# Fewer, larger units of half-array products in a mixer layer, and selector products filled from 36 to 128 rows

## The chip, the core and the metric

The kernel runs on one core of one Trainium2 chip. Its engines work side by side, each through its own list of instructions in order: TensorE (PE in the profile; its weight loads are PEld), VectorE (DVE), ScalarE (ACT), GpSimd (POOL), and SyncE (SP), which issues most DMAs. The metric is the device time of one execution in microseconds (us). Three runs of the kernel before took 302.65, 302.69 and 302.83 us.

## The reference

One decoder layer on a sequence of 512 tokens of width 1024, all float32:

- RMS norm of x, then one projection `h @ w_in` to 4616 columns, and at the end one projection `y @ w_out` back to 1024, added to x.
- A matrix-memory group (mLSTM) of 4 heads of width 128: causal convolution and SiLU on q and k, input and forget gates, a stabilised recurrence over time, a norm per head, a SiLU gate.
- An attention group of 8 heads of width 64: norm of q and k, a linear penalty on distance, softmax over all earlier keys, a SiLU gate. With 512 tokens and blocks of 256, the "top 3 blocks" are all the past there is, so this is plain causal attention.

```
s = q . k * scale - slope * distance      (masked to the past)
p = softmax(s);   o = p @ v
y = concat(h_mlstm * silu(z_ml), o * silu(z_at)) @ w_out;   return x + y
```

## The kernel before

**Products in parts.** A float32 operand of the large products is split into a high part (`whi`, `xh`) and a remainder (`wlo`, `xl`), and a product becomes three fast ones, high x high, high x low and low x high. ACT makes the high part of a weight tile, DVE the remainder; PE then streams 512 columns per product through the full array of 128 rows x 128 columns. "Wide product" below means one of these.

**Attention.** `g_attn` works on a pair of heads, 2p and 2p+1, that lie in rows 0 to 63 and 64 to 127 of the same tiles (four tiles named `br`: high and low parts of q and k). A *query tile* is 128 query rows; there are four. For tile i, `g_tile` (L861) takes two PSUM banks, one for each head, and issues six score products, three for each head in turn: rows 0 to 63 of the array for the one, rows 64 to 127 for the other, so that the two run at the same time. Width is 256, 256, 384 and 512 columns for tiles 0 to 3. In `g_soft` DVE adds the penalty and takes the row's extreme (a custom instruction, named CUSTOM_DVE_ANT_0), ACT exponentiates, DVE inverts the sum, POOL scales. PE turns the probabilities over (128x128 products with the identity, `ident`), and four steps of probabilities times values (L923) follow: 64 columns of the array for each head, two heads at a time. These are plain float32 products, and each has two records in the trace.

**Matrix memory.** `g_mlstm` (L982) needs for each head a row of running maxima copied to all 128 partitions. It does this as a product of `sel` (a matrix of zeros and ones) with `mrow2` (L989): both have 36 rows, of which rows 0 to 3 and 32 to 35 matter. There are four such selector products.

**What sets the order.** At the start the program writes constants by hand: POOL makes `ident`, `dist`, clears `mrow2` and the edge of `xp`; DVE clears a tile for ten warm-up products of zeros on PE and adds up `sel` from pieces of `ident`. These are issued in the order of the code. From `nc.on = True` (L647) on, instructions are only recorded. `Schedule` then gives each a cost and a list of what it must follow (tiles read and written; a PSUM bank counts as a whole), places them engine by engine, backwards and forwards twelve times (`place`, L308), and issues them in the order of the best placing. What is recorded between `nc.bundle = []` and `nc.bundle = None` is one unit (L262): it is placed as one and nothing of PE's comes in between. All instructions of the recorded part carry the line of their issue, L258, so they are told apart by tile names. `tables` (L292) keeps ACT's Exp, SiLU and Sigmoid work in the order of the recording and puts a table load between.

**Banks.** `banks` has eight PSUM banks; `KEEP = 3` is what a recorded program leaves free for the main stream of wide products.

Of the kernel before, what the change touches and what calls it, by code (L numbers as in the profile page):

```python
# [11 lines left out]
F32 = mybir.dt.float32  # L12
# [5 lines left out]
P = 128  # L18
# [171 lines left out]
class Schedule:  # L190
# [61 lines left out]
    def add(self, eng, name, fn, args, kw):  # L252
        aps = [a for a in (*args, *kw.values()) if isinstance(a, bass.AP)]
        out = kw.get("out", args[0] if args else None)
        outs = [r for r in (self.region(a) for a in (out, kw.get("accum_out")) if a is not None) if r]
        ins = [r for r in (self.region(a) for a in aps if a is not out and a is not kw.get("accum_out")) if r]
        dma = name.startswith("dma")
        call = lambda: fn(*args, **kw)  # L258
        op = {"eng": eng, "fn": [call], "cost": self.cost(eng, name, out, ins, args, kw), "n": len(self.ops),
              "table": next((self.TABLES[a] for a in args if isinstance(a, AF) and a in self.TABLES), 0) if name == "activation" else 0,  # L260
              "pre": {}}
        if self.bundle is not None:  # L262

            if not self.bundle:
                self.bundle.append(op)
            elif op is not self.bundle[0]:
                self.bundle[0]["cost"] += op["cost"]
                self.bundle[0]["fn"].append(call)
            op = self.bundle[0]
        if op["n"] == len(self.ops):  # L270
            self.ops.append(op)
        done = op
        if dma:
            size = 4.0
            for d in out.shape:
                size *= d
            done = {"eng": "dma", "fn": None, "cost": size / 524288.0 * (2900.0 if kw.get("accum_op") else 1480.0), "n": len(self.ops),
                    "table": 0, "pre": {op["n"]: 0.0}}
            self.ops.append(done)
        for reg, write in [(r, False) for r in ins] + [(r, True) for r in outs]:  # L280
            log = self.log.setdefault(reg[0], [])
            for r, w, o in log:
                if (w or write) and r[1] < reg[2] and reg[1] < r[2] and r[3] < reg[4] and reg[3] < r[4]:
                    if o["n"] in (op["n"], done["n"]):
                        continue
                    lat = self.LAT[o["eng"]] if o["eng"] != eng else 0.0 if eng == "tensor" else self.OWN if w else 0.0
                    op["pre"][o["n"]] = max(op["pre"].get(o["n"], 0.0), lat)
            if write:
                log[:] = [e for e in log if e[2] in (op, done) or not (reg[1] <= e[0][1] and e[0][2] <= reg[2] and reg[3] <= e[0][3] and e[0][4] <= reg[4])]
            log.append((reg, write, done))  # L290
# [97 lines left out]
def hybrid_layer(ctx: ExitStack, tc: tile.TileContext, xT, x, w_in, w_out, smalls, out):  # L388
# [11 lines left out]
    def sb(name, shape, dtype=F32):  # L400
        return const.tile(shape, dtype, name=name)
# [10 lines left out]
    def pe(t=0.0, cond=None):  # L412
        return (t, cond, True)
# [8 lines left out]
    def mm(out_, lhsT, rhs, start=True, stop=True):  # L422
        n = 1
        for d in rhs.shape[1:]:
            n *= d
        plan.now += n / 2.4 if rhs.dtype == F32R else 4 * max(n, 128) / 2.4
        nc.tensor.matmul(out_, lhsT=lhsT, rhs=rhs, start=start, stop=stop, skip_group_check=True)
# [192 lines left out]
    rstd = sb("rstd", [P, NT])  # L620
    acol = sb("acol", [P, NT, 4])
    emcol = sb("emcol", [P, NT, 4])
    mrow2 = sb("mrow2", [36, S], F32R)
    nc.gpsimd.memset(mrow2.bitcast(F32), 0.0)
    sel = sb("sel", [36, MLH, P], F32R)
    for h in range(MLH):
        nc.vector.tensor_tensor(sel[:, h], ident[0:36, h:h + 1].to_broadcast([36, P]),
                                ident[0:36, 32 + h:33 + h].to_broadcast([36, P]), op=ALU.add)
    xpt = sb("xp", [P, 2, S + 4])
    nc.gpsimd.memset(xpt[:, :, 0:3], 0.0)  # L630
# [216 lines left out]
    def g_attn(p, qh, ql, kh, kl, t0):  # L847
        rank = 5 + p / 100
        yield when(lambda: b2.ok() and b5.ok(2) and (p < 2 or 2 * p - 3 in pts))
        eh, prs = b2.get(), [b5.get() for _ in range(2)]  # L850

        te = pool.tensor_scalar(eh, dist, 2.0 ** -(2 * p + 1), 0.0, op0=ALU.mult, op1=ALU.add)
        mn, sums, rec = ([tiny(NT) for _ in range(2)] for _ in range(3))
        done = {"p": [0, 0], "t": [0, 0]}
        at = [t0, t0]

        def finish(key, u, t):
            at[u] = max(at[u], t)
            done[key][u] += 1

        def g_tile(i):  # L861
            n = P * (i + 1)
            nn = max(n, 256)
            yield (max(*at, te), lambda: banks.ok(KEEP + 1), True)
            ps = [banks.get() for _ in range(2)]
            ts = slice(i * P, (i + 1) * P)
            now = plan.now
            nc.bundle = []
            for a, b in ((qh, kh), (qh, kl), (ql, kh)):
                for u in range(2):  # L870
                    r = slice(64 * u, 64 * u + 64)
                    mm(ps[u][:, :nn], a[r, ts], b[r, :nn], a is qh and b is kh, a is ql)
            nc.bundle = None
            plan.now = (now + plan.now) / 2
            for u in range(2):
                plan.add(g_soft(u, i, n, ps[u]), rank, plan.now + SLACK)

        def g_soft(u, i, n, ps):
            p_ = prs[u][:, offs[i]:offs[i] + n]
            t_ = dve.tensor_tensor_reduce(p_, ps[:, :n], eh[:, S - n:], scale=-0.5 if u else -1.0, scalar=BIG,  # L880
                                          op0=ALU.add, op1=ALU.min, accum_out=mn[u][:, i:i + 1])
            banks.put(t_, ps)
            yield t_
            yield act.activation(p_, p_, AF.Exp, scale=-1.0, bias=mn[u][:, i:i + 1], accum_out=sums[u][:, i:i + 1])
            have["exp"] += 1
            dve.reciprocal(rec[u][:, i:i + 1], sums[u][:, i:i + 1])
            yield dve.clock + SLACK
            finish("p", u, pool.tensor_scalar(p_, p_, rec[u][:, i:i + 1], 1.0, op0=ALU.mult, op1=ALU.mult))

        def g_pt(u, a, blocks, pt):  # L890
            yield pe_bank(at[u])
            ps = banks.get()
            n = P * len(blocks)
            for b, (i, j) in enumerate(blocks):
                transpose(ps[:, b * P:(b + 1) * P], prs[u][:, offs[i] + j * P:offs[i] + (j + 1) * P], ident)
            yield plan.now + SLACK
            t_ = (act.copy, dve.tensor_copy, act.copy)[a](pt[:, 512 * a:512 * a + n], ps[:, :n])
            banks.put(t_, ps)
            finish("t", u, t_)

        def g_turn(u):
            yield when(lambda: done["p"][u] == NT and b5.ok())
            pt = b5.get()
            for a, blocks in enumerate(([(0, 0), (1, 0), (2, 0), (3, 0)],
                                        [(1, 1), (2, 1), (3, 1), (3, 3)],
                                        [(2, 2), (3, 2)])):
                plan.add(g_pt(u, a, blocks, pt), rank)
            yield when(lambda: done["t"][u] == 3)
            b5.put(plan.now, prs[u])
            pts[2 * p + u] = (pt, [pt[:, 0:512], pt[:, 512:896], pt[:, 1024:1280], pt[:, 896:1024]], at[u])  # L910

        for i in range(NT):
            plan.add(g_tile(i), rank)
        for u in range(2):
            plan.add(g_turn(u), rank + u / 200)
        yield when(lambda: sum(done["p"]) == 2 * NT)
        b2.put(plan.now, eh)
        br.put(plan.now, qh, ql, kh, kl)
        h = 2 * p + 1
        yield when(lambda: h in pts and h - 1 in pts and have["v"] == NT)  # L920
        yield pe_bank(max(pts[h][2], pts[h - 1][2]))
        acc = banks.get()
        for j in range(NT):  # L923
            nc.bundle = []
            for g in (h - 1, h):
                r0 = 64 * (g % 2)
                mm(acc[r0:r0 + 64, j * P:], tv[:, j, g * 64:g * 64 + 64], pts[g][1][j], j == 0, j == NT - 1)
            nc.bundle = None
            plan.now -= 4 * (S - j * P) / 2.4
            if j < NT - 1:  # L930
                yield pe()
        b5.put(plan.now, pts[h - 1][0], pts[h][0])
        yield plan.now + SLACK
        banks.put(dve.tensor_copy(ot[:, h // 2], acc), acc)
        have["at"] += 1
# [694 lines left out]
```

## Time and profile before

| | us |
|---|---|
| median of three runs | 302.69 |
| the profiled execution, its own time | 302.68 |
| its span, first to last instruction | 301.0 |
| PE busy | 296.0 (98%) |
| DVE busy | 214.9 (71%) |
| ACT busy | 169.6 (56%) |
| POOL busy | 67.1 (22%) |

Between span and own time lie 1.7 us. A product's end is modelled and products overlap in the array, so PE counts as busy whenever its products follow each other, whether at full pace or not. Its pace is read from the starts: from one start to the next. The attention of all heads lies between 96.6 and 178.8 us of the span, the selector products between 170.7 and 173.1.

### The profile page before, as it was taken

Reading aid. Unit: us, or ns where it says so; the run is one execution under the profiler, and the core shown is the slowest. Engines: PE = TensorE matmul, PEld = TensorE weight load, DVE = VectorE, ACT = ScalarE, POOL = GpSimd, SP = SyncE. Lnnn points to the kernel's source line nnn. Section 1 sums busy time; section 2 is a strip of 40 time slices with the busy share of each in tenths; the row PEclk is TensorE's granted clock in tenths of the full one; section 3 lists DMA queues with packets and bytes.
Section 4 is the critical chain, followed back from the end, with each engine's and each line's share of the span. In section 5 each row is a group of like instructions: output and inputs, shape, how many; then the busy total and the mean of one; then the engine's idle time right before and its main releaser. Section 6 shows DMA issues by size and latency. Waiting matters only on the chain.

```text
span 301.0 us, 4348 instructions
## 1 busy us (share of the span) xinstructions
PE 296.0 (98%) x1566; PEld 234.9 (78%) x1566; DVE 214.9 (71%) x457; ACT 169.6 (56%) x309; POOL 67.1 (22%) x90
## 2 busy tenths in 40 slices
PE   8999999999999999999999999999999999999995
PEld 3999888888887667767776668888889988888884
DVE  4886996789697675986686784372046767899992
ACT  3685749875537854364554599377032525779500
POOL 4000202149900344002561031000101037121200
PEclk9999999999999999999999999999999999999998
DMA  7994785643134200240001601465518399964434
GB/s 203 396 415 186 191 237 148 121 138 114 58 111 140 71 2 0 70 142 1 1 3 70 209 2 70 70 207 154 131 42 212 102 286 255 247 112 74 71 127 153
DMA packets 13381, 40.19 MB, mean 134 GB/s; under 512 B 1584, under 2 KB 1840, under 8 KB 13360
## 3 DMA queue, kind: packets, MB, share of 16 engines
q1 hardware_dynamic: 10640, 32.05, 30.6%
q0 software_dynamic: 2720, 7.87, 15.3%
q8 instruction: 12, 0.20, 0.3%
q14 instruction: 9, 0.07, 0.1%
HBM read 37.81 MB, written 2.10 MB: 133 GB/s over the span
## 4 chain that ended last, share of the span: by engine, by line
PE 97%; DMA 1%; DVE 0%; SPq 0%; issue 0%
PE bank L258 97%; DMA b<-in_w_in_dram 1%; DVE whi L258 0%; DVE b L258 0%; SPq L258 0%; SPq L381 0%
## 5 line engine op out<-in xcount | busy, mean ns | idle before, releaser
L258 PE MATMUL bank<-wlo,xh 128*128 128x512 f32 (+2 forms) x220 | 71.3, 358 | 0.0
L258 PE MATMUL bank<-whi,xl 128*128 128x512 f32 (+2 forms) x220 | 71.1, 359 | 0.0
L258 PE MATMUL bank<-whi,xh 128*128 128x512 f32 (+2 forms) x220 | 70.9, 362 | 0.1
L258 DVE TENSOR_TENSOR wlo<-raw,whi 128x1024 fp32r<-128x1024 f32 x35 | 42.5, 1218 | 22.3 <-ACT whi L258 22.2
L258 PEld LDWEIGHTS bank<-whi,xh 128*128 128x128 f32 x220 | 38.1, 188 | 8.1 <-ACT xh L258 1.0
L258 PEld LDWEIGHTS bank<-wlo,xh 128*128 128x128 f32 x220 | 38.3, 188 | 6.6 <-issue 0.2
L258 PEld LDWEIGHTS bank<-whi,xl 128*128 128x128 f32 x220 | 38.3, 188 | 6.4
L258 ACT CAST whi<-raw 128x1024 fp32r<-128x1024 f32 x35 | 36.5, 1049 | 11.6 <-PE bank L258 11.5
L258 PE MATMUL bank<-xh,whi 128*128 128x512 f32 x96 | 40.8, 425 | 0.0
L258 PE MATMUL bank<-xl,whi 128*128 128x512 f32 x96 | 39.4, 410 | 0.0
L258 PE MATMUL bank<-xh,wlo 128*128 128x512 f32 x96 | 38.7, 403 | 0.0
L258 PE MATMUL bank<-whi,br 128*128 128x512 f32 x112 | 35.9, 397 | 0.0
L258 POOL TENSOR_SCALAR b<-b,tinies 128x128 f32<-128x128 f32 (+3 forms) x32 | 20.0, 632 | 35.1 <-DVE tinies L258 32.5
L258 PEld LDWEIGHTS bank<-whi,br 128*128 128x128 f32 x112 | 21.0, 188 | 5.0
L258 ACT ACTIVATE b<-b,tinies 128x128 f32<-128x128 f32 (+3 forms) x32 | 17.8, 556 | 11.3 <-DVE tinies L258 11.0
L258 DVE CUSTOM_DVE_ANT_0 b<-bank,b 128x128 f32<-128x128 f32 (+3 forms) x32 | 14.8, 483 | 10.7 <-PE bank L258 10.7
L258 PEld LDWEIGHTS bank<-xh,whi 128*128 128x128 f32 x96 | 18.1, 188 | 5.5 <-issue 1.4
L258 PE MATMUL bank<-wlo,br 128*128 128x512 f32 x56 | 22.2, 400 | 0.0
L258 PEld LDWEIGHTS bank<-xh,wlo 128*128 128x128 f32 x96 | 18.1, 188 | 3.8 <-issue 0.2
L258 PEld LDWEIGHTS bank<-xl,whi 128*128 128x128 f32 x96 | 18.1, 189 | 3.6 <-issue 0.7
L258 POOL TENSOR_TENSOR tinies<-tinies,mhalf 128x8 f32<-128x8 f32 (+1 forms) x12 | 18.9, 1589 | 6.3 <-DVE tinies L258 6.2
L258 PE MATMUL bank<-ident,b 128*128 128x128 f32 (+1 forms) x104 | 19.0, 267 | 0.0
(170 smaller groups left out, 457.2 us busy)
## 6 DMA issues: line engine op xcount, KB each, us to landing
raw<-in_w_in_dram SPq DMA_DIRECT2D x28, 512.0 KB, 3.4
raw<-in_w_out_dram SPq DMA_DIRECT2D x5, 512.0 KB, 4.4
vbuf<-in_x_dram SPq DMA_DIRECT2D x4, 512.0 KB, 7.8
out_dram<-b SPq DMA_DIRECT2D x7, 256.0 KB, 2.1
b<-in_w_in_dram SPq DMA_DIRECT2D x3, 520.0 KB, 7.1
raw<-in_w_out_dram POOLq DMA_DIRECT2D x3, 512.0 KB, 6.3
b<-in_x_dram POOLq DMA_DIRECT2D x6, 256.0 KB, 4.4
tq<-in_xT_dram SPq DMA_DIRECT2D x4, 256.0 KB, 4.9
```

The lines of the kernel that those rows point to most:

```text
L258: call = lambda: fn(*args, **kw)
```

## The change

Three edits. `g_tiles` puts the scores of two query tiles into one unit, (0, 1) and (2, 3); tiles 0 and 1 share one bank for each head (columns 0 to 255 and 256 to 511), tiles 2 and 3 take two banks for each head at once. A shared bank is given back after both reductions have read it. The four steps of probabilities times values become one unit. `sel` and `mrow2` get 128 rows; the new rows are zero, so `sel` is cleared on POOL before DVE adds into its first 36 rows. Besides, the planner charges each unit 190 ns more.

```diff
@@ Schedule.add
             if not self.bundle:
                 self.bundle.append(op)
+                op["cost"] += 190.0
@@ hybrid_layer
-    mrow2 = sb("mrow2", [36, S], F32R)
+    mrow2 = sb("mrow2", [P, S], F32R)
     nc.gpsimd.memset(mrow2.bitcast(F32), 0.0)
-    sel = sb("sel", [36, MLH, P], F32R)
+    sel = sb("sel", [P, MLH, P], F32R)
+    nc.gpsimd.memset(sel.bitcast(F32), 0.0)
     for h in range(MLH):
-        nc.vector.tensor_tensor(sel[:, h], ident[0:36, h:h + 1].to_broadcast([36, P]),
+        nc.vector.tensor_tensor(sel[0:36, h], ident[0:36, h:h + 1].to_broadcast([36, P]),
                                 ident[0:36, 32 + h:33 + h].to_broadcast([36, P]), op=ALU.add)
@@ g_attn
-        def g_tile(i):
-            n = P * (i + 1)
-            nn = max(n, 256)
-            yield (max(*at, te), lambda: banks.ok(KEEP + 1), True)
-            ps = [banks.get() for _ in range(2)]
-            ts = slice(i * P, (i + 1) * P)
+        def g_tiles(tiles):
+            n_banks = 1 if tiles[0] == 0 else 2
+            yield (max(*at, te), lambda: banks.ok(KEEP + 2 * n_banks - 1), True)
             now = plan.now
-            nc.bundle = []
-            for a, b in ((qh, kh), (qh, kl), (ql, kh)):
-                for u in range(2):
-                    r = slice(64 * u, 64 * u + 64)
-                    mm(ps[u][:, :nn], a[r, ts], b[r, :nn], a is qh and b is kh, a is ql)
+            nc.bundle, got = [], []
+            for j, i in enumerate(tiles):
+                n = P * (i + 1)
+                nn = max(n, 256)
+                if j < n_banks:
+                    ps = [banks.get() for _ in range(2)]
+                c0 = 0 if j < n_banks else 256
+                ts = slice(i * P, (i + 1) * P)
+                for a, b in ((qh, kh), (qh, kl), (ql, kh)):
+                    for u in range(2):
+                        r = slice(64 * u, 64 * u + 64)
+                        mm(ps[u][:, c0:c0 + nn], a[r, ts], b[r, :nn], a is qh and b is kh and not c0, a is ql)
+                got.append((i, n, ps, c0))
             nc.bundle = None
...
-            banks.put(t_, ps)
+            left[id(ps)] -= 1
+            if not left[id(ps)]:
+                banks.put(t_, ps)
...
-        for i in range(NT):
-            plan.add(g_tile(i), rank)
+        for tiles in ((0, 1), (2, 3)):
+            plan.add(g_tiles(tiles), rank)
...
         acc = banks.get()
+        nc.bundle = []
         for j in range(NT):
-            nc.bundle = []
             for g in (h - 1, h):
                 r0 = 64 * (g % 2)
                 mm(acc[r0:r0 + 64, j * P:], tv[:, j, g * 64:g * 64 + 64], pts[g][1][j], j == 0, j == NT - 1)
-            nc.bundle = None
             plan.now -= 4 * (S - j * P) / 2.4
-            if j < NT - 1:
-                yield pe()
+        nc.bundle = None
```

The diff leaves the order to the planner, so three places are shown as the built programs have them.

PE, the first scores of heads 0 and 1, before: `br` tiles are q and k, each `bank` a PSUM bank; `xh`, `xl`, `whi0`, `wlo0` belong to a wide product.

```order
L258 MATMUL bank2_82<-xl_107,whi0_108 128x512
L258 MATMUL bank0_80<-br_2_74,br_0_72 128x256
L258 MATMUL bank3_83<-br_2_74,br_0_72 128x256
L258 MATMUL bank0_80<-br_3_75,br_0_72 128x256
L258 MATMUL bank3_83<-br_3_75,br_0_72 128x256
L258 MATMUL bank0_80<-br_2_74,br_1_73 128x256
L258 MATMUL bank3_83<-br_2_74,br_1_73 128x256
L258 MATMUL bank2_82<-xh_106,wlo0_109 128x512
L258 MATMUL bank7_87<-br_2_74,br_0_72 128x384
L258 MATMUL bank5_85<-br_2_74,br_0_72 128x384
L258 MATMUL bank7_87<-br_3_75,br_0_72 128x384
L258 MATMUL bank5_85<-br_3_75,br_0_72 128x384
```

The same place of the change, from the last products of tile 1 over tile 2 into tile 3:

```order
L258 MATMUL bank6_86<-br_3_75,br_0_72 128x256
L258 MATMUL bank4_84<-br_2_74,br_1_73 128x256
L258 MATMUL bank6_86<-br_2_74,br_1_73 128x256
L258 MATMUL bank0_80<-br_2_74,br_0_72 128x384
L258 MATMUL bank3_83<-br_2_74,br_0_72 128x384
L258 MATMUL bank0_80<-br_3_75,br_0_72 128x384
L258 MATMUL bank3_83<-br_3_75,br_0_72 128x384
L258 MATMUL bank0_80<-br_2_74,br_1_73 128x384
L258 MATMUL bank3_83<-br_2_74,br_1_73 128x384
L258 MATMUL bank7_87<-br_2_74,br_0_72 128x512
L258 MATMUL bank5_85<-br_2_74,br_0_72 128x512
L258 MATMUL bank7_87<-br_3_75,br_0_72 128x512
```

Before, a wide product stands between tile 0, tile 1 and tile 2; now all 24 score products of this pair of heads stand in one piece.

PE, the selector products (`mrow2` and `sel`), before:

```order
L258 MATMUL bank1_81<-mrow2_149,sel_151 128x512
L258 MATMUL bank0_80<-ident_124,b5_4_67 128x128 x2
L258 MATMUL bank5_85<-ident_124,b5_4_67 128x128
L258 MATMUL bank3_83<-mrow2_149,sel_151 128x512
L258 MATMUL bank7_87<-mrow2_149,sel_151 128x512
L258 MATMUL bank6_86<-whi0_108,xh_106 128x512
L258 MATMUL bank2_82<-mrow2_149,sel_151 128x512
```

They stand in three pieces, and of the change in two:

```order
L258 MATMUL bank6_86<-whi3_114,xl_107 128x512
L258 MATMUL bank0_80<-mrow2_149,sel_151 128x512
L258 MATMUL bank1_81<-mrow2_149,sel_151 128x512
L258 MATMUL bank7_87<-whi0_108,xh_106 128x512
L258 MATMUL bank7_87<-wlo0_109,xh_106 128x512
L258 MATMUL bank7_87<-whi0_108,xl_107 128x512
L258 MATMUL bank5_85<-mrow2_149,sel_151 128x512
L258 MATMUL bank4_84<-mrow2_149,sel_151 128x512
```

The piece matters less here than the rows: the products now fill the array's 128 rows, as their neighbours do.

POOL, the constants at the start, of the change (before has the same rows without the fill of `sel`, and 36 rows in that of `mrow`):

```order
masks.py:199 AFFINE_SELECT ident<-ident 128x128
L382 MEMSET mhalf 128x8
L382 IOTA dist 128x512
L382 AFFINE_SELECT dist<-dist 128x512
L382 MEMSET one_col 128x1
L382 MEMSET mrow_149 128x512
L382 MEMSET sel 128x512
L382 MEMSET xp 128x2x3
```

DVE at the start, of the change (before has the same rows): the four additions into `sel`, and behind them the first high part of weights.

```order
L382 MEMSET rstdb 128x256
L382 MEMSET warm 128x1
L382 TENSOR_TENSOR sel<-ident 36x128 x4
L258 CAST whi_108<-b_0_63 128x520
L258 SCALAR_TENSOR_TENSOR xl<-tq,sm,xh 128x512
```

The additions read only `ident` before; now they also follow POOL's fill of `sel`, which stands five rows behind `ident` there.

## Rows read from the trace of the kernel before

**Rows 1.** Stretch and its us; busy PE, PEld, DVE, ACT, POOL; clock, DMA share, GB/s.

```profile
96.60:178.80 82.20, 82.20 (x467) 56.67 (x466) 59.53 (x166) 46.98 (x122) 23.16 (x38) 1.00 0.16 52
```

**Rows 2.** Everything that PE waited for: engine, line, releaser, us, times, longest.

```profile
PE bank L381 <- DVE warm L381: 1.2, 1, 1.2
```

**Rows 3.** Chain that ended last, its longest piece: start, us, what.

```profile
5.83 291.52 PE bank L258 x1556
```

**Rows 4.** Timeline of PE, tiles 2 and 3 of heads 2, 3: start, us, what.

```profile
106.10 0.40 PE L258 MATMUL bank<-xh,wlo 128*128 128x512 f32 x1
106.43 0.79 PE L258 MATMUL bank<-br,br 64*128 64x384 f32 x6
107.15 0.50 PE L258 MATMUL bank<-xh,whi 128*128 128x512 f32 x1
107.48 0.39 PE L258 MATMUL bank<-xl,whi 128*128 128x512 f32 x1
...
107.94 0.40 PE L258 MATMUL bank<-xh,whi 128*128 128x512 f32 x1
108.27 0.96 PE L258 MATMUL bank<-br,br 64*128 64x512 f32 x6
109.16 0.50 PE L258 MATMUL bank<-xl,whi 128*128 128x512 f32 x1
109.50 0.39 PE L258 MATMUL bank<-xh,wlo 128*128 128x512 f32 x1
```

**Rows 5.** Timeline of PE, tiles 2 and 3 of heads 6, 7, which adjoin.

```profile
150.77 0.40 PE L258 MATMUL bank<-xh,wlo 128*128 128x512 f32 x1
151.10 1.49 PE L258 MATMUL bank<-br,br 64*128 64x384 f32 x12
152.52 0.50 PE L258 MATMUL bank<-xh,whi 128*128 128x512 f32 x1
152.85 0.39 PE L258 MATMUL bank<-xl,whi 128*128 128x512 f32 x1
```

**Rows 6.** Timeline of PE, the last selector product.

```profile
172.25 0.49 PE L258 MATMUL bank<-whi,xh 128*128 128x512 f32 x1
172.67 0.50 PE L258 MATMUL bank<-mrow,sel 36*128 36x512 f32 x1
173.10 0.50 PE L258 MATMUL bank<-wlo,xh 128*128 128x512 f32 x1
173.44 0.39 PE L258 MATMUL bank<-whi,xl 128*128 128x512 f32 x1
```

**Rows 7.** Timeline of PE, wide products between steps of probabilities times values.

```profile
176.80 0.50 PE L258 MATMUL bank<-whi,xh 128*128 128x512 f32 x1
177.13 0.39 PE L258 MATMUL bank<-wlo,xh 128*128 128x512 f32 x1
```

**Rows 8.** Timeline of POOL at the start.

```profile
3.20 0.29 POOL masks.py:199 TENSOR_SCALAR_AFFINE_SELECT ident<-ident 128x128 f32<-128x128 f32 x1
...
4.88 0.51 POOL L381 MEMSET mrow<- 36x512 f32 x1
5.34 0.38 POOL L381 MEMSET xp<- 128x6 f32 x1
```

**Rows 9.** Timeline of DVE at the start.

```profile
3.52 0.89 DVE L381 TENSOR_TENSOR sel<-ident 36x128 fp32r<-36x128 f32 x4 [2.33 <-POOL ident masks.py:199]
5.16 0.53 DVE L258 CAST whi<-b 128x520 fp32r<-128x520 f32 x1 [0.74 <-DMA b<-in_w_in_dram]
```

**Rows 10.** Timeline of PE, the warm-up products.

```profile
1.24 4.45 PE L381 MATMUL bank<-rstdb 128*128 128x512 bf16 x10 [1.24 <-DVE warm L381]
```

**Rows 11.** Groups by form (count | busy, mean ns | idle before): score reductions, table loads.

```profile
L258 DVE CUSTOM_DVE_ANT_0 b<-bank,b 128x256 f32<-128x256 f32 x8 | 3.2, 422 | 4.2 <-PE bank L258 4.2
L258 DVE CUSTOM_DVE_ANT_0 b<-bank,b 128x128 f32<-128x128 f32 x8 | 2.0, 282 | 1.8 <-PE bank L258 1.8
...
L258 ACT ACT_TABLE_LOAD x4 | 5.1, 1283 | 0.1
```

More of the change, by code (lines that the diff above doesn't have):

```diff
@@ L873, in g_tile @@
             nc.bundle = None
             plan.now = (now + plan.now) / 2
-            for u in range(2):
-                plan.add(g_soft(u, i, n, ps[u]), rank, plan.now + SLACK)
-        def g_soft(u, i, n, ps):
+            left = {}
+            for _, _, ps, _ in got:
+                for u in range(2):
+                    left[id(ps[u])] = left.get(id(ps[u]), 0) + 1
+            for i, n, ps, c0 in got:
+                for u in range(2):
+                    plan.add(g_soft(u, i, n, ps[u], c0, left), rank, plan.now + SLACK)
@@ L879, in g_soft @@
+        def g_soft(u, i, n, ps, c0, left):
             p_ = prs[u][:, offs[i]:offs[i] + n]
-            t_ = dve.tensor_tensor_reduce(p_, ps[:, :n], eh[:, S - n:], scale=-0.5 if u else -1.0, scalar=BIG,
+            t_ = dve.tensor_tensor_reduce(p_, ps[:, c0:c0 + n], eh[:, S - n:], scale=-0.5 if u else -1.0, scalar=BIG,
                                           op0=ALU.add, op1=ALU.min, accum_out=mn[u][:, i:i + 1])
-            banks.put(t_, ps)
+            left[id(ps)] -= 1
+            if not left[id(ps)]:
+                banks.put(t_, ps)
```

## The prediction

> **What bounds the kernel now.** I read the busy times by stretch first, then what PE waited for, then the chain that ended last, and only then the timeline. In the attention's stretch PE has a product in it for 82.20 of 82.20 us while DVE, ACT and POOL have gaps [rows 1]. Over the whole execution PE waited for another engine once, for DVE at the very start [rows 2], and the chain that ended last is one unbroken piece of 1556 products on PE from 5.83 us on [rows 3]. So the time is the sum of PE's steps from one start to the next, plus the moment of its first real product. Everything else can only matter by making PE late.
>
> The steps are not all alike. Wide products next to each other start 0.23 us apart; around scores, which use half of the array's rows each, the steps are longer. Tile 2 and tile 3 of heads 2 and 3 stand alone: wide to score takes 0.33 us (106.10 to 106.43, and 107.94 to 108.27), and the step after the first wide product behind scores 0.33 and 0.34 [rows 4]. The six scores of tile 2 hold PE for 0.72 us and those of tile 3 for 0.89, together 1.61. The same two tiles of heads 6 and 7 happen to stand together and take 1.42 (151.10 to 152.52) [rows 5]. So the trace already holds the change in small: two pieces cost 4 edges and one piece 2.
>
> **The price of one piece.** From the wide product at 106.10 to the one at 107.48 are 1.38 us, less two wide steps of 0.23 leaves 0.92 for tile 2; from 107.94 to 109.50 are 1.56, less the same leaves 1.10 for tile 3: 2.02 [rows 4]. From 150.77 to 152.85 are 2.08, less 0.46 leaves 1.62 for both in one piece [rows 5]. One piece less is worth 0.40 us. It is made of some 0.10 each for the first score, the last score, the step into the piece and the step behind it.
>
> **What the change removes.** Counted over PE's whole order, pieces of scores fall from 15 to 7. The four pairs of heads had 16 units, two of which adjoin; now there are 8 units, two of which adjoin (heads 0 and 1). 8 x 0.40 = 3.2 us.
>
> The selector products stood in three pieces. From the wide product at 172.25 to that at 173.44 are 1.19 us for two wide products and one selector product: three plain steps are 0.69, and 0.50 is left, 0.10 of which is the step behind the piece before it. So a piece of these costs 0.40 too [rows 6]. With 128 rows the products use the array as the wide ones do, and no edge should remain: 3 x 0.40 = 1.2 us.
>
> Of probabilities times values two of the four pairs of heads had their steps in two pieces, now none: 6 pieces become 4. Behind such a piece the first wide step is 0.33 us again [rows 7]; the other edges I price as those of scores, with 0.10 as the lower and 0.40 as the upper end for a piece. I take 0.40, since the one edge seen equals that of scores: 0.8 us (0.2 to 0.8).
>
> The sum of gains is 5.2 us. The number of products is the same, 1474 in both orders, and so are their widths.
>
> **What it adds at the start.** This is where the change costs. Before, DVE's four additions into `sel` began at 3.52 us, 0.03 behind the end of POOL's `ident` (3.20 + 0.29), and were done at 4.41. DVE's next instruction, the high part of the first weights, began at 5.16, when its DMA had landed; it had 0.74 us to spare [rows 8, 9]. Now the additions write into a tile that POOL has to clear first. In POOL's list that fill stands behind the fill of `mrow`, which took from 4.88 to 5.34, where the next one began [rows 8]. So the new fill begins at 5.34 at best. It has as many columns as that of `mrow`, whose 0.51 us I take for it; the trace has no fill of 128 rows and this width, and `xp`'s six columns took 0.38, so it lies between 0.38 and, if time went by rows, four times 0.51, which is 2.0. It ends at 5.85, the additions run from 5.88 to 6.77, and the high part starts at 6.77 in place of 5.16: 1.6 us later (1.5 to 3.1). DVE works in order, so nothing behind can pass. PE's first real product needs that high part, and the 1556 products behind it never wait again, so the whole delay comes through to the end. Queued behind the additions on DVE are, besides that high part, the low parts of x and of the weights, all of which PE takes as they come. On POOL the fill of `xp` and one small instruction come half a microsecond later; nobody waits for them then.
>
> **What is hidden.** A reduction of tile 0 now waits for tile 1 as well, and a shared bank comes free after two reductions of each head instead of one: 2 x (0.28 + 0.42) = 1.4 us of DVE work [rows 11]. In the new order 13 wide products follow the first 24 scores before the next pair of heads takes these banks, 13 x 0.23 = 3.0 us. DVE is idle for 22.7 of the 82.2 us there [rows 1]. I take nothing for it; uncovered it would cost up to 1.4 us at each of four places. ACT's list gets one more table load, 1.28 us [rows 11], since SiLU now stands between the exponentials of two matrix-memory heads and those of the other two. ACT has 35 us free in this stretch [rows 1], and the first turned product of the matrix memory stands 45 wide products (10 us) behind the last selector product; nothing, with 1.3 as the upper end. The last 160 rows of PE's list are the same, so the end should follow PE as before.
>
> **Sum.** 302.68 (the profiled execution, against a median of 302.69) - 3.2 - 1.2 - 0.8 + 1.6 = 299.1 us.
>
> **The rivals.**
>
> *The fill costs nothing* (the additions are early enough all the same, or DVE's first high part is not held): then 302.68 - 5.2 = 297.5. For it speaks only that DVE had 0.74 us to spare; against it that the fill begins 0.18 us after the moment at which that instruction began.
>
> *The clock comes back late.* The ten warm-up products took 4.45 us, 0.43 for 512 columns [rows 10], twice the 0.23 of the wide products later [rows 4]: by their pace they ran at the lower of PE's two levels, 1.2 GHz, and the first real products followed 0.14 us behind them, after which the trace shows the higher pace. Now PE would stand still from 5.69 to about 7.4 us. If a stretch as long as the warm-up then ran at the lower level again, it would lose half of 4.45, 2.2 us: 301.3. For it: the whole warm-up ran at the lower level. Against it: the warm-up itself is unchanged, and the pause is little more than a third of it. The Trainium skill (TensorE: Matmul & The Clock Gate, What's actually happening) says that the throttled state is the default and that activity releases it, which makes idling at this place the dangerous kind. The trace agrees in so far as the ten products did run at half pace.
>
> *Only part of the price goes away*, because a piece with 128 rows of zeros or two tiles in one bank pays its edges all the same: half of the gain, 302.68 - 2.6 + 1.6 = 301.7. Against it are the two adjoining tiles [rows 5].
>
> *Slower: PE waits for the banks.* With four banks for each unit of tiles 2 and 3, and shared ones for 0 and 1, PE could stand at the start of each pair's units until DVE has reduced the tiles before. If PE waits out all the reductions of two shared banks, 1.4 us, twice at each of four pairs of heads, it loses 11.2 us: 310.3. It decides from 3.6 us on, which is 0.9 for each pair. For it: banks are held longer, and DVE is at 72% there. Against it: before, PE never waited for DVE [rows 2], and the planner knows the banks.
>
> **How the numbers follow.** The likeliest case, 299.1 and within 298.4 to 300.1, has 0.63; the fill for nothing 0.09; the late clock, anywhere between 299.7 and 301.3 since the rise may come halfway, 0.16; half of the price 0.05; waits for banks 0.07, of which 0.04 end above the time before. A measurement of this kernel tells about 0.2% (0.6 us) from no change. Faster by more than that needs a time under 302.1: all cases but the waits and a piece of the longest fill, 0.90; within 0.2%: 0.05; slower: 0.05. The range goes from 298.0, which leaves out the fill for nothing, to 301.3, which takes in the late clock and leaves out half of the price and the waits: 0.2 outside.
>
> **What would show it.** In the profile after: PE's first real product at about 7.4 us, with DVE's `sel` additions from 5.9 and the fill of `sel` on POOL just before them; 24, 12, 12, ... score products in seven pieces, and the step into a piece 0.33 as before; a selector product 0.23 us behind its neighbour; all 16 records of a pair's probabilities times values in one piece; PE without a wait between its first product and its last; and a span shorter by 3.5. It would be wrong if the first product still came at 5.8, if products at about 7.4 to 12 us ran at half pace, or if PE waited for DVE between 100 and 110 us.

## The result, and the profile after

Four runs took 298.98, 300.04, 300.50 and 300.50 us, median 300.27, against 302.67 for the kernel before in the same runs: ratio 0.991 (95% interval 0.989 to 0.993). The profiled execution is the one of 298.98, against 302.68 for the profiled one before: 3.7 us less. The other three are 1.1 to 1.5 us longer, and no run of the kernel before is spread like that (302.20 to 302.83). Their mean granted clock is 0.994 in both runs of 300.50 and 0.998 in that of 300.04, against 0.999 in the profiled one; none of the three has a profile.

The chain that ended last, after (start, us, what):

```profile
0.79 1.84 DMA sm<-in_smalls_dram
...
4.83 0.46 POOL mrow L382
5.29 0.46 POOL sel L382
5.75 0.05 POOL xp L382
5.80 0.06 DVE sel L382
...
6.01 0.68 DVE sel L382 x3
6.69 0.35 DVE whi L258
...
7.18 286.48 PE bank L258 x1556
```

Two numbers carry the result. PE's piece is 286.48 us in place of 291.52 [rows 3], 5.04 less for the same 1556 products. And it starts at 7.18 in place of 5.83, 1.35 later, because the chain now runs through POOL's fills and DVE's additions to the first high part of weights; before, that part waited for its DMA [rows 8, 9]. 5.04 - 1.35 is the 3.7. DVE's own timeline shows the additions behind the fills (`xp` is the POOL instruction that follows the fill of `sel`) and the high part right behind them:

```profile
5.78 0.91 DVE L382 TENSOR_TENSOR sel<-ident 36x128 fp32r<-36x128 f32 x4 [4.59 <-POOL xp L382]
6.62 0.41 DVE L258 CAST whi<-b 128x520 fp32r<-128x520 f32 x1
```

PE stood still for 1.5 us in this execution too, and yet it went on at the higher pace: the first eight products took 1.18 us (7.18 to 8.36), as long as before, and the granted clock behind them is 1.00 (below, a stretch with its busy times, clock, DMA share and GB/s).

```profile
7.18 1.19 PE L258 MATMUL bank<-whi,xh 128*128 128x264 f32 x8 [1.50 <-DVE whi L258]
9.00:10.00 1.00, 1.00 (x10) 1.00 (x10) 1.00 (x3) 0.00 (x0) 0.00 (x0) 1.00 1.02 395
```

Timeline of PE after, the first scores (the piece of 24 is both units of heads 0 and 1; that of 12 is tiles 0 and 1 of heads 2 and 3), and below the selector products and the last probabilities times values:

```profile
98.09 0.39 PE L258 MATMUL bank<-xl,whi 128*128 128x512 f32 x1
98.41 2.20 PE L258 MATMUL bank<-br,br 64*128 64x256 f32 x24
100.54 0.50 PE L258 MATMUL bank<-xh,wlo 128*128 128x512 f32 x1
100.87 0.39 PE L258 MATMUL bank<-xh,whi 128*128 128x512 f32 x1
...
103.76 0.98 PE L258 MATMUL bank<-br,br 64*128 64x256 f32 x12
104.67 0.50 PE L258 MATMUL bank<-xh,whi 128*128 128x512 f32 x1
...
174.29 0.62 PE L258 MATMUL bank<-mrow,sel 128*128 128x512 f32 x2
174.75 0.40 PE L258 MATMUL bank<-whi,xh 128*128 128x512 f32 x1
174.98 0.39 PE L258 MATMUL bank<-wlo,xh 128*128 128x512 f32 x1
...
176.70 2.37 PE L258 MATMUL bank<-b,vbuf 128*64 128x512 f32 x16
179.00 0.50 PE L258 MATMUL bank<-whi,xh 128*128 128x512 f32 x1
```

The edges are as dear as before: 98.09 to 98.41 is 0.32, 100.54 to 100.87 is 0.33, as in [rows 4]. There are fewer of them. The first two selector products take 0.46 from 174.29 to 174.75, two plain wide steps, where one took 0.43 and left its neighbours longer [rows 6].

What PE waited for, after (engine, line, releaser: us, times, longest):

```profile
PE bank L258 <- DVE whi L258: 1.5, 1, 1.5
PE bank L382 <- DVE warm L382: 1.2, 1, 1.2
```

The new row against [rows 2] is the start; no wait for a bank or a softmax appears. The attention's stretch again holds a product on PE for its whole length, with DVE 6.6 us busier in the same window than in [rows 1]:

```profile
96.60:178.80 82.20, 82.20 (x489) 61.56 (x488) 66.11 (x174) 48.29 (x119) 28.00 (x36) 1.00 0.20 66
```

### The profile page after: what moved, and what is told of

Read it like the earlier page. It is cut to its first block, busy times and chain, and to the rows that moved or that the text cites. A ratio compares the mean times of both kernels' runs of the same rounds, so it can differ in the third digit from the quotient of the medians.

```text
span 297.3 us, 4346 instructions
## 1 busy us (share of the span) xinstructions
PE 290.9 (98%) x1566; PEld 235.7 (79%) x1566; DVE 215.0 (72%) x457; ACT 170.0 (57%) x310; POOL 74.8 (25%) x91
## 4 chain that ended last, share of the span: by engine, by line
PE 96%; POOL 1%; DMA 1%; DVE 1%; issue 0%; POOLq 0%
PE bank L258 96%; DMA sm<-in_smalls_dram 1%; POOL dist L382 0%; DVE sel L382 0%; POOL mrow L382 0%; POOL sel L382 0%; DVE b L258 0%; DVE whi L258 0%; POOL ident masks.py:199 0%; POOL ident masks.py:197 0%; POOL sm L382 0%; POOL mhalf L382 0%; POOL xp L382 0%; POOL one_col L382 0%; POOLq L382 0%
## 5 line engine op out<-in xcount | busy, mean ns | idle before, releaser
L258 PE MATMUL bank<-xh,whi 128*128 128x512 f32 x96 | 40.2, 419 | 0.0
L258 PE MATMUL bank<-xl,whi 128*128 128x512 f32 x96 | 38.5, 401 | 0.0
L258 POOL TENSOR_SCALAR b<-b,tinies 128x128 f32<-128x128 f32 (+3 forms) x32 | 24.5, 776 | 38.3 <-DVE tinies L258 38.2
L258 POOL TENSOR_TENSOR tinies<-tinies,mhalf 128x8 f32<-128x8 f32 (+1 forms) x12 | 20.8, 1746 | 6.6 <-DVE tinies L258 6.5
L258 PE MATMUL bank<-ident,b 128*128 128x128 f32 (+1 forms) x104 | 17.4, 268 | 0.0
```

## The experiments

The theory: PE is bound by its own steps; each change between the full array and a part of it costs some 0.2 us (a piece has two); the late fill of `sel` delays PE's first product; and the runs above 299 come from the clock, which rises late behind the pause that the delay makes. The rivals: the price belongs to units or kinds of product and not to the changes; the start has slack; the spread comes from the new order.

**The fill moved to where POOL is free** (label early_fill):

```diff
+    sel = sb("sel", [P, MLH, P], F32R)
+    nc.gpsimd.memset(sel.bitcast(F32), 0.0)
     nc.gpsimd.tensor_scalar(sm[64:128, C_QW:C_QW + 1], ...
...
-    sel = sb("sel", [P, MLH, P], F32R)
-    nc.gpsimd.memset(sel.bitcast(F32), 0.0)
```

> The changed kernel with POOL's fill of sel moved ahead of its first instruction, where POOL is free; order of PE unchanged. Theory (the edges of the pieces give 5.0 us, the late fill costs 1.35 at PE's first product, and the rest of the distance between the profiled 298.98 and the median 300.27 is a clock that rises late behind the pause): first product at 5.8 us as before, every run within 0.3 of 297.5, granted clock near 0.998 in each. Rival (the slower runs come from the new order, not from the pause): first product at 5.8, but runs still spread over 1.5 us, median near 298.9.

Measured: 297.88 us (297.82 to 297.92 in four runs), ratio to the kernel before 0.984 (0.982 to 0.985). POOL's timeline (start, us) shows the fill in idle time, DVE's that the additions are back at their old place:

```profile
0.79 0.53 POOL L382 MEMSET sel<- 128x512 f32 x1 [0.29 <-POOLq L1631]
2.62 0.18 POOL L382 TENSOR_SCALAR sm<-sm 64x1 f32<-64x1 f32 x1 [1.31 <-DMA sm<-in_smalls_dram]
```

```profile
3.47 0.89 DVE L382 TENSOR_TENSOR sel<-ident 36x128 fp32r<-36x128 f32 x4 [2.28 <-POOL ident masks.py:199]
5.46 0.43 DVE L258 CAST whi<-b 128x520 fp32r<-128x520 f32 x1 [1.09 <-DMA b<-in_w_in_dram]
```

The high part waits for its DMA again. The spread shrank from 1.5 to 0.1 us with PE's order untouched, so the order is not its cause. In that the theory's outcome came, and the level did not: every run is 0.32 to 0.42 above the expected 297.5, where at most 0.3 was expected. In the profiled run 0.2 of it is a DMA that landed later (first product at 6.04 in place of 5.83); the rest has no source in these rows.

**The late fill alone** (late_fill_only; the kernel before and one line):

```diff
     sel = sb("sel", [36, MLH, P], F32R)
+    nc.gpsimd.memset(sel.bitcast(F32), 0.0)
```

> The kernel before with nothing but a fill of sel (36 rows) on POOL behind that of mrow2; no unit is joined. Theory: the first product moves from 5.8 to 7.2 us, the time to 304.0 at least (302.67 + 1.35), and in runs where the clock rises late to 305.5. Rival (the start has slack after all, and the change simply gained less in its pieces): within 0.4 of 302.7.

Measured: 305.29 us (303.85 to 305.50 in six runs), 2.5 us slower than before, ratio 1.0072 (1.0057 to 1.0087). One run, 303.85, paid no more than the delay (1.1 above the kernel before); five were 1.2 to 1.7 longer than that one. The profiled one (305.50) shows PE's first product at 7.13 and a piece of 293.06 us for the order that took 291.52 before [rows 3]:

```profile
1.24 4.27 PE L381 MATMUL bank<-rstdb 128*128 128x512 bf16 x10 [1.24 <-DVE warm L381]
7.13 1.19 PE L258 MATMUL bank<-whi,xh 128*128 128x264 f32 x8 [1.61 <-DVE whi L258]
```

Where the 1.5 us lie is seen in its windows (stretch, us; busy PE, PEld, DVE, ACT, POOL; granted clock, DMA share, GB/s):

```profile
7.00:8.00 1.00, 0.87 (x7) 0.90 (x8) 1.00 (x2) 0.61 (x1) 0.00 (x0) 1.00 0.90 356
8.00:9.00 1.00, 1.00 (x7) 0.80 (x6) 1.00 (x3) 0.00 (x0) 0.00 (x0) 0.81 1.04 389
9.00:10.00 1.00, 1.00 (x7) 1.00 (x7) 1.00 (x3) 0.00 (x0) 0.00 (x0) 0.50 1.05 393
...
11.00:12.00 1.00, 1.00 (x7) 1.00 (x6) 1.00 (x2) 0.68 (x1) 0.00 (x0) 0.50 1.07 414
12.00:13.00 1.00, 1.00 (x10) 1.00 (x10) 1.00 (x2) 0.78 (x1) 0.00 (x0) 0.99 1.01 410
```

The granted clock falls to one half, 1.2 GHz, within the ninth microsecond, stays there to about 12, and a microsecond then touches 7 products in place of 10. Ahead of the fall PE had stood still from 5.51, the end of its warm-up, to 7.13. The Trainium skill (TensorE: Matmul & The Clock Gate, What's actually happening) says that the throttled state is the default and that activity releases it; this trace agrees, with 0.50 behind a pause of 1.6 us. The profile of the change had a pause of 1.5 us and no such fall, so in some executions the fall follows such a pause and in others it does not.

**A longer warm-up** (longer_warm; the changed kernel, fill still late):

```diff
-    for _ in range(10):
+    for _ in range(14):
         nc.tensor.matmul(wb, lhsT=zero[:, 0:P], rhs=zero, start=True, stop=True)
```

> The changed kernel with 14 warm-up products in place of 10, so that PE works on zeros until shortly before its first real product; the fill of sel stays late. Theory (late clock behind the pause): the first product stays at 7.2 us, every run is within 0.3 of 299.0 and none shows a clock of 0.994. Rival (the spread has another cause): runs at 300.0 to 300.5 as often as with the change, median 300.2.

Measured: 298.95 us (298.88 to 299.03 in four runs). Timeline of PE at its start:

```profile
1.24 4.66 PE L382 MATMUL bank<-rstdb 128*128 128x512 bf16 x14 [1.24 <-DVE warm L382]
7.03 1.20 PE L258 MATMUL bank<-whi,xh 128*128 128x264 f32 x8 [1.13 <-DVE whi L258]
```

With the delay in place and four more products of zeros, the spread is gone. The pause is shorter too (5.90 to 7.03), and the fourteen took only 0.2 us longer than ten did [rows 10], so part of them ran at the higher level. More work ahead and a shorter pause came together here; the run doesn't say which of the two helped. PE's order and its piece (286.51 us) are those of the change's profile, and the first product came 0.15 earlier; most of the 1.3 us to the change's median is thus what its longer runs lost. That it was the clock is seen in two of those three (0.994); for the third, 300.04, it is not shown.

**The selector products on 36 rows again** (sel36; early_fill with one line changed, the same order on PE):

```diff
-        mm(ps, sel[:, h], mrow2)
+        mm(ps, sel[0:36, h], mrow2[0:36])
```

> As early_fill, but the selector products take only rows 0 to 35 again: the same order on PE, four products in two pieces with the array switched to half its rows. Theory (0.40 us for each piece): 0.8 us slower than early_fill, 298.3. Rival (what counts is how many units PE changes between, not the rows of the array): the same as early_fill within 0.2.

Measured: 298.78 us (298.45 to 299.31), 0.9 more than early_fill, with four changes of the array more. Timeline of PE around the second of the two pieces:

```profile
174.38 0.39 PE L258 MATMUL bank<-whi,xl 128*128 128x512 f32 x1
174.70 0.73 PE L258 MATMUL bank<-mrow,sel 36*128 36x512 f32 x2
175.35 0.50 PE L258 MATMUL bank<-whi,xh 128*128 128x512 f32 x1
175.69 0.40 PE L258 MATMUL bank<-wlo,xh 128*128 128x512 f32 x1
```

0.32 into the piece, 0.65 inside in place of 0.46, 0.34 behind it. Nothing but the number of rows differs, so the rows are the price and not the unit.

**Each part alone, and one step further.** `sel128_alone` takes only the 128 rows (with the early fill), `pv_alone` only the joined probabilities times values, `scores_alone` only the joined scores, all on the kernel before; their diffs are those parts of the change (without the 190 ns, which no run takes or leaves by themselves). `four_tiles` is early_fill with

```diff
-            n_banks = 1 if tiles[0] == 0 else 2
-            yield (max(*at, te), lambda: banks.ok(KEEP + 2 * n_banks - 1), True)
+            yield (max(*at, te), lambda: banks.ok(7), True)
...
-                if j < n_banks:
+                if i != 1:
...
-                c0 = 0 if j < n_banks else 256
+                c0 = 256 if i == 1 else 0
...
-        for tiles in ((0, 1), (2, 3)):
+        for tiles in ((0, 1, 2, 3),):
```

> The kernel before with 128 rows in sel and mrow2 alone, the fill of sel early so that the start stays as it was; units and order as before. Theory (0.2 us for each time the array changes between full and part): 6 changes fewer (49 to 43), 301.6. Rival (the selector products were not slow for their rows): 302.7.

> The kernel before with the four steps of probabilities times values in one unit, nothing else. The planner makes a new order from it, in which the array changes 44 times in place of 49. Theory (0.2 us for each change): 301.8. Rival (a long unit delays what stands behind it): 302.7 or more, with waits of PE.

> The kernel before with the scores of two query tiles in one unit, nothing else, without the 190 ns. In the planner's new order scores stand in 8 pieces, but steps of probabilities times values in 9 (6 before); the array changes 40 times. Theory (each change 0.2 us, whatever it is between): 301.0. Rival (the sum by kinds, as the prediction made it: 8 units fewer are worth 3.2 us by themselves): 299.6.

> As early_fill, with the scores of all four query tiles of a pair of heads in one unit of 24 products (six banks held). The array changes 5 times less (23 to 18). Theory (edges only): 297.88 - 1.0 = 296.9, PE without waits. Rival (the forecast's slower case: PE now waits for banks): 298 or more, with waits of PE for DVE between 100 and 160 us.

The table has the median of each, PE's piece in its profile (the row that stands for the kernel before in [rows 3]), and how often the array changes between full and part, or from one kind of part to another, in PE's order (the count includes the eight products of 4 rows). In the rounds of these runs the kernel before took 302.67 to 302.76; the profiled execution of the change is its fastest:

| kernel | changes | PE's piece, us | median, us |
|---|---|---|---|
| before | 49 | 291.52 | 302.75 |
| pv_alone | 44 | 291.09 | 301.93 |
| sel128_alone | 43 | 290.38 | 301.64 |
| scores_alone | 40 | 289.56 | 300.81 |
| sel36 | 27 | 287.33 | 298.78 |
| the change | 23 | 286.48 | 300.27 |
| early_fill | 23 | 286.54 | 297.88 |
| longer_warm | 23 | 286.51 | 298.95 |
| four_tiles | 18 | 285.62 | 296.70 |

From 49 to 23 changes PE's piece loses 5.04 us, 0.19 for each, and the others lie near that line, but for pv_alone, which lost 0.43 where it gives 1.0. Its start shows where the rest went (the first two lines are of pv_alone, the others of the kernel before):

```profile
5.71 1.89 PE L258 MATMUL bank<-whi,xh 128*128 128x264 f32 x8
7.43 1.12 PE L258 MATMUL bank<-wlo,xh 128*128 128x264 f32 x8
5.83 1.24 PE L258 MATMUL bank<-whi,xh 128*128 128x264 f32 x8
7.01 1.22 PE L258 MATMUL bank<-wlo,xh 128*128 128x264 f32 x8
```

The same eight products took 1.72 us (5.71 to 7.43) in place of 1.18, so 0.54 of PE's piece was lost at a lower pace that has nothing to do with changes; without it the piece lies on the line.

scores_alone decides between the theory and the sum by units joined: eight units of scores fewer should have given 299.6, and by changes 301.0; it took 300.81, since the planner's new order has the steps of values in 9 pieces (6 before) with the scores in 8. Counting the pieces of the built order at 0.40 us would do as well: 24 before (15, 3 and 6), 19 here (8, 2 and 9), so 2.0 us less, 300.8.

The three parts alone save 5, 6 and 9 changes, 20 in all, and 3.9 us together. All of them with the early fill save 26 changes and 4.9 us: the rest lies in the order that the planner makes of them together.

four_tiles is the fastest version, ratio to the kernel before 0.980 (0.979 to 0.981). Its waits of PE, and its first piece:

```profile
PE bank L382 <- DVE warm L382: 1.2, 1, 1.2
PE bank L258 <- DVE whi L258: 0.9, 1, 0.9
```

```profile
97.99 0.39 PE L258 MATMUL bank<-xh,whi 128*128 128x512 f32 x1
98.31 2.21 PE L258 MATMUL bank<-br,br 64*128 64x256 f32 x24
100.44 0.50 PE L258 MATMUL bank<-xl,whi 128*128 128x512 f32 x1
...
106.22 2.20 PE L258 MATMUL bank<-br,br 64*128 64x256 f32 x24
```

Even with six banks in one unit PE waits for no bank: 5.8 us of wide products lie between the pieces of two pairs of heads.

## Why the prediction was right or wrong

- *What bounds it.* Right: the time is PE's steps plus the moment of its first product, in every kernel here.
- *The price of a piece and what is removed.* Right: 5.2 forecast, 5.04 measured in PE's piece. Counting pieces gave the same as counting changes, since 13 pieces are 26 changes; scores_alone shows that the count has to be made in the built order and not from the units that the code joins.
- *The delay at the start.* Right in mechanism, over by 0.25: 1.6 forecast, 1.35 measured. The fill of 128 rows took no longer than that of 36 had [rows 8], 0.46 from its start to the next in the chain, and what stands ahead of it on POOL ended a little sooner. So the high part that follows the additions began at 6.62, not 6.77, 0.07 before their end, and it took 0.41 in place of 0.53 [rows 9].
- *What is hidden.* Right: no wait of PE for banks, and the fifth table load on ACT was not seen on PE. The rival of waits for banks fell with the change, and with four_tiles where it had most reason.
- *The chances.* These were weighed wrongly. The forecast, 299.1, is what the change takes when the clock holds: 298.98 in one run of four, 298.95 with the longer warm-up. The median lies 1.2 above, in the range of the case "the clock comes back late", which was given 0.16 and 299.7 to 301.3; the measured gain is 2.4 us where 3.6 was forecast, and the stated range holds it only because it took that case in. Such longer runs were the usual ones: three of four here, five of six with the late fill alone. The argument against the case was the ratio of the pause to the warm-up, and no row says that a pause of that size leaves the clock as it is.
- *The mechanism of that case* was put as a late rise. In the one profile that has a loss behind the pause, late_fill_only's, the clock had been high and fell. By its pace, pv_alone's profile has a late rise, and without a pause: its first product follows the warm-up at once (5.71), the first eight go slowly and the next do not, while the record reads a clock of 1.00. Of the five longer runs of late_fill_only, two show a mean granted clock of 0.992 and three read 1.00. Whether in those three, or in the change's run of 300.04, the clock rose late is open, since the record reads 1.00 during the warm-up too, whose products go at the pace of 1.2 GHz [rows 10].

## What to carry to other kernels

When PE is never idle, look at the steps from one start to the next: here every change between the full array and a part of it costs 0.19 us, and a planner that does not know of it scatters small products for nothing. Count the changes in the built order, not the units, since joining one kind can break up another. And a constant written at the start is not free because it is small: place it by what is queued behind it on its engine, since in late_fill_only 1.30 us of delay became 2.5 us, the rest of it, where a profile shows it, from the clock.

## What the runs showed of the hardware

- A fill of 512 columns on POOL takes 0.53 us for 128 rows (early_fill's timeline) and 0.51 for 36 [rows 8].
- The Trainium skill (TensorEngine Tiling (Array Packing), Tiling Modes, Key Properties) says that changing the tiling mode drains TensorE. The runs agree in so far as every such change costs time, and give a size: 0.19 us for each, in four parts of some 0.1 for a piece, seen alike for products of 64 rows, of 36 rows and of 64 columns. Two units of different kinds that adjoin pay one change between them, not two. In the change's profile values and scores adjoin at 137.03, and each takes what it takes alone, 2.30 us (as from 176.70 to 179.00) and 0.91 (as from 103.76 to 104.67), with no wide step of 0.33 between them:

```profile
134.73 2.37 PE L258 MATMUL bank<-b,vbuf 128*64 128x512 f32 x16
137.03 0.98 PE L258 MATMUL bank<-br,br 64*128 64x256 f32 x12
137.94 0.50 PE L258 MATMUL bank<-xh,whi 128*128 128x512 f32 x1
```

- In late_fill_only's profile a pause of 1.6 us behind the warm-up was followed by a granted clock of 0.50 from about 8.6 to 12 us. The change's profile, with a pause of 1.5 us, and those with one of 1.1 us or less do not show it.
- The clock column can read 1.00 while PE works at the lower pace: during the warm-up [rows 10] and at pv_alone's first eight products, 0.215 us each in place of 0.148.
